# A streaming encoder step: strip products in longer groups, value products between feature tiles, sums off TensorE, and other planning margins

## The chip, the cores and the metric

The kernel runs on one core of a Trainium2 chip, as one launch. TensorE (PE) multiplies matrices, VectorE (DVE), ScalarE (ACT) and GpSimd (POOL) do the elementwise work, and DMA queues, issued by SyncE (SP) and GpSimd, move data between HBM and the core's own memory. The metric is the device time of one execution in microseconds (us).

## The reference, cut to what matters

Two layers of an encoder trunk are evaluated for 256 prompt tokens and for 8 streams of 16 sample tokens. Together these are 384 token rows of 1024 features.

```python
for i in range(2):
    x = x + 0.5 * rms(swiglu(rms(x), ffn 1))
    x = x + rms(conformer_conv(rms(x)) if i == 0 else gated_deltanet(rms(x)))
    x = x + rms(memory_cross_attention(rms(x), mem_k[i], mem_v[i]))
    x = x + 0.5 * rms(swiglu(rms(x), ffn 2))

def conformer_conv(h):                  # layer 0's mixer
    val, gate = split(h @ w_in + b_in)  # 1024 features each
    u = val * sigmoid(gate)
    c = depthwise_conv(u, 31 taps) + dw_b
    c = silu(layer_norm(c))             # mean and variance over the 1024 features
    return c @ w_out + b_out

def memory_cross_attention(h, k, v):    # 4 heads of 256, 256 memory tokens
    return softmax((h @ wq) k^T / 16) v @ wo
```

The memory keys and values of the prompt (`mem_prompt @ xa_wk`, `mem_prompt @ xa_wv`, both layers) are outputs too. The sample streams have their own keys and values, read from caches. The delta mixer of layer 1 keeps a 128 x 128 state per head and stream. All data is fp32.

## The kernel before, in words

Token tile 0 holds the 8 sample streams, tiles 1 and 2 the prompt. Each weight comes from HBM as a chunk of 128 x 1024 (`get`): SyncE loads it to `raw`, ScalarE copies it to `whi` in the type fp32r, and VectorE subtracts to get the rest, `wlo`. For chunks named in `SLOW`, GpSimd does that subtraction. A product is then three passes, high by high, high by low and low by high. Activations are split likewise into `hTh` and `hTl` (the normed input, turned so that features lie on partitions) and `rbh` and `rbl`. Products in plain fp32, such as the prompt's keys, are one product in the code and two matmul records in the trace. They stand as `ps<-big`.

Python generators emit operations with rough costs, and `Scheduler` orders all of them. It knows a cost for each operation, a delay from engine to engine (`LAT`), slots for DMAs, and then fixes one order for each engine. `early` places operations forwards by priority, `late` backwards; passes alternate, and the best end is kept. An engine on the chip runs its own order without exception and waits where data is late. So constants in the planner change the order and nothing else.

The names that the change touches:

- `quad` emits a set of four products side by side in four strips of 32 columns of the array (L265 in the trace), since each sample stream has its own keys. A head of the cross-attention has four sets for the scores and four for the values (two groups of streams, two halves of the contraction). A head of the delta mixer has two, for the state. Before, each set is an operation of its own to the planner, which may put other products between sets.
- `conv` emits eight feature tiles (a gate product `cg` and a value product `cv`, 24 passes of 384 columns each), then `glu` for each. The task `taps` takes the tiles in pairs: 31 taps each on VectorE, accumulated in PSUM. After each pair two products with a matrix of 1/1024 (`onesd`) add to the mean.
- `ln` normalises one token tile: subtract the mean (VectorE), square (ScalarE), eight products with `onesd` for the variance, power on GpSimd, a product that broadcasts it, multiply, SiLU.
- `kv_split` makes the prompt's values, as eight units of 48 passes of 256 columns, each with two weight chunks `v2`. It first splits the memory into `rbh` and `rbl`. Before, it runs behind the eighth feature tile.
- `kv(n)` emits n key products (each eight fp32 products of 256 columns) at places given by `KV`, where TensorE would wait for the norms between blocks.
- `chain` is the norm between two blocks, with its transposes on TensorE (L285).

Of the kernel before, what the change touches and what calls it, by code (L numbers as in the profile page):

```python
# [11 lines left out]
ALU = mybir.AluOpType  # L12
# [3 lines left out]
P = 128  # L16
D = 1024
KT = 8
NTOK = 384
# [17 lines left out]
RUSH = 10000.0  # L37
FIRST_SLOW = 2
ORD = 12000.0
# [5 lines left out]

KV = {"start": 3, "f00": 3, "conv": 5, "co": 2, "xo": 0, "f01": 1, "f10": 2, "dn": 0, "f11": 0}
HALF = 1400.0
GROUPS = [(0, 1), (2, 3, 4, 5, 6, 7)]
TAIL = 3
PASSES = 3  # L50
POOLTRUE = 1
LANES = 8
DMA_IN, DMA_OUT = 650.0, 950.0
# [47 lines left out]
class Emitter:  # L101
# [154 lines left out]
    def quad(self, mms):  # L256

        n = self._n(mms[0][2])
        cost = 2 * max(107.0, n / 1.2) + 190.0
        self.vt += cost  # L260
        t = self.nc.tensor

        def go():
            for out, lhsT, rhs, start, stop in mms:
                t.matmul(out, lhsT, rhs, start=start, stop=stop)  # L265
        self._add("P", cost, go, [x for m in mms for x in m[1:3]], [m[0] for m in mms])
        return self.vt + HOP
# [55 lines left out]
class Scheduler:  # L323

    LAT = {"P": {"P": 0, "A": 197, "V": 197}, "A": {"P": 275, "V": 131, "G": 159, "A": 131},
           "V": {"P": 260, "A": 128, "V": 127, "G": 155}, "G": {"P": 311, "A": 77, "V": 76, "G": 104}}

# [112 lines left out]
    def early(self, prio):  # L442
# [12 lines left out]
        for _ in ops:  # L455
            best, e, i = self.pick(free, now, later, lambda i: -prio[i])
            o = ops[i]
            cost = o.cost
            if o.nbytes:
                best = max(best, lanes[e][0])  # L460
            at[i] = best
            if o.table and o.table != table:
                table = o.table
                cost += 1283.0
            end = free[e] = best + cost
            if o.nbytes:
                dma = max(dma, end + DMA_IN) + o.nbytes / 360.0
                end = dma + DMA_OUT
                lanes[e] = lanes[e][1:] + [end]
            last = max(last, end)  # L470
            for j in o.succ:
                rd[j] = max(rd[j], end + (0.0 if o.nbytes else self.LAT[e].get(ops[j].eng, 150)))
                npred[j] -= 1
                if not npred[j]:
                    heapq.heappush(later[ops[j].eng], (rd[j], j))
# [66 lines left out]
class Model:  # L542
# [399 lines left out]
    def kv_split(self):  # L942


        E = self.E
        vt = E.vt
        mh, ml = (a.rearrange("p k c -> p (k c)")[:, 0:2 * D] for a in (self.rbh, self.rbl))
# [13 lines left out]
        for l in range(2):  # L961
            for h in range(XH):

                o, b = self.bank()
# [14 lines left out]
                self.bfree(b)  # L979
                E.store(self.O["pkv"][l, h][:, 512:1024], r)  # L980
        self.free(rh)
        E.vt = vt

# [76 lines left out]
    def conv(self, chains, post, pre):  # L1060
# [31 lines left out]

        def taps():
            for c0 in range(0, KT, 2):
                cs = (c0, c0 + 1)
# [24 lines left out]
                self.bfree(ab)  # L1120
                if not means:
                    means.append((yield from self.gbank()))
                for c in cs:
                    self.free(hist[c][1], hist[c][3])
                    E.mm(means[0][0][:, 0:NTOK], self.onesd, cO[:, c, :], c == 0, c == KT - 1)
            self.conv_end = e

        means = []
        tapper = E.spawn(taps())
        prefetch(0)  # L1130
        prefetch(1)
        for c in range(KT):
# [9 lines left out]
            if c + 2 < KT:  # L1142
                prefetch(c + 2)

        self.kv_split()
        self.kv(KV["conv"])
# [8 lines left out]
        def ln(t, dep):  # L1155
# [10 lines left out]
            yield e - 300  # L1166
            e = E.act(qv, x, AF.Square, dep=e)
            yield e
            o, b = yield from self.gbank()
            for k in range(KT):  # L1170
                e = E.mm(o[:, 0:P], qv[:, k, :], self.onesd, k == 0, k == KT - 1)
            v, r = self.st(1), self.st(1)
# [33 lines left out]
    def xattn(self, l, chains, post, pre):  # L1206
        E = self.E
# [14 lines left out]
        def head(h):  # L1222
# [3 lines left out]
            pk = unit[h, "p"][0]  # L1226
            sc, scb = yield from self.gbank2()
            for g in range(2):
                for c in range(2):
                    q4 = []  # L1230
                    for j in range(4):
# [3 lines left out]
                                   c == 0, c == 1))  # L1235
                    e0 = E.quad(q4)
            for t in (1, 2):
# [32 lines left out]
            yield max(e, e1, unit[h, ("v", 3)][2])  # L1270
            pv, pvb = yield from self.gbank2()
            for g in range(2):
                for m in range(2):
                    q4 = []
                    for j in range(4):
# [3 lines left out]
                        q4.append((pv[0][32 * j:32 * j + 32, g * MEM:(g + 1) * MEM], pt[:, o:o + 32], vv, m == 0, m == 1))  # L1279
                    e0 = E.quad(q4)  # L1280
            for d in range(2):
# [80 lines left out]
    def deltanet(self, chains, post, pre):  # L1362
# [119 lines left out]
        def head(h, q, k, v):  # L1482
# [136 lines left out]
            o, b = yield from self.gbank()  # L1619
            for n, a in ((0, kT), (256, qT)):  # L1620
                e = E.quad([(o[32 * j:32 * j + 32, n:n + 256], a[:, 32 * j:32 * j + 32], S[:, 256 * j:256 * j + 256], True, True)
                            for j in range(4)])

# [300 lines left out]
```

## Time and profile before

| | us |
|---|---|
| median of three runs | 1880.22 (1877.89 to 1883.22) |
| the profiled execution | 1880.99 |
| its span, first to last instruction | 1879.2 |
| PE busy | 1848.6 (98%) |
| DVE busy | 986.4 (52%) |
| ACT busy | 765.5 (41%) |
| POOL busy | 252.6 (13%) |

The stages on the span are: first feed-forward to about 305, convolution to about 512, first cross-attention to about 626, two feed-forwards to about 1186, delta mixer to about 1480, second cross-attention to about 1600, last feed-forward.

In the profile, a row of the timeline gives start, length, engine, line, operation, what is written and read, shape, count, and in brackets the idle time of the engine before it and what ended it. Matmuls overlap, so a single one's length is longer than the time until the next may start. That time is read from start to start.

### The profile page before, as it was taken

What the parts mean: (1) busy time and instruction counts of PE and PEld (TensorE: products, weight loads), DVE (VectorE), ACT (ScalarE), POOL (GpSimd) and SP (SyncE); (2) the same over time, 40 slices, a digit from 0 to 9 for tenths busy, and PEclk for the clock granted to TensorE, in tenths of its full rate; (3) what the DMA queues carried; (4) which work ended last, traced back from release to release, by engine and by line L of the source; (5) the groups of instructions that cost most, each with busy time, mean ns of one, the idle gap of its engine ahead of it and who ended that gap; (6) DMA issues with size and microseconds to landing.
All of it is one profiled execution on the core that took longest, in us unless ns stands there. A gap on an engine that the chain in (4) does not pass through costs nothing.

```text
span 1879.2 us, 26770 instructions
## 1 busy us (share of the span) xinstructions
PE 1848.6 (98%) x10479; PEld 1658.3 (88%) x10479; DVE 986.4 (52%) x1681; ACT 765.5 (41%) x1443; POOL 252.6 (13%) x420
## 2 busy tenths in 40 slices
PE   8999999999999999999999999999999999999998
PEld 7988998998877799999899999899998777899997
DVE  5456335898542643333643333687877644533333
ACT  4332334334542532323533333676665544432332
POOL 1000003568100100000200000233231101000000
PEclk9999999999999999999999999999999999999999
DMA  8534435448487534444434344333334583534441
GB/s 303 163 119 128 135 113 148 128 141 258 165 302 275 153 113 129 128 124 134 155 114 128 120 131 124 107 102 104 103 118 154 193 328 108 157 124 124 135 123 45
DMA packets 88622, 279.81 MB, mean 149 GB/s; under 512 B 17904, under 2 KB 20464, under 8 KB 88496
## 3 DMA queue, kind: packets, MB, share of 16 engines
q1 hardware_dynamic: 86368, 272.47, 45.4%
q0 software_dynamic: 2128, 5.63, 0.9%
q8 instruction: 82, 1.34, 0.3%
q14 instruction: 44, 0.36, 0.1%
HBM read 266.14 MB, written 11.92 MB: 148 GB/s over the span
## 4 chain that ended last, share of the span: by engine, by line
PE 63%; ACT 2%; DVE 2%; DMA 1%; POOL 1%; issue 1%; DVEq 0%; POOLq 0%; ACTq 0%; SPq 0%
PE ps L253 60%; PE ps L265 2%; PE ps L285 2%; DMA raw<-in_w 1%; DVE wlo L203 1%; ACT big L196 1%; POOL stat L203 1%; DVE big L216 1%; ACT whi L195 1%; PE ps L278 0%; ACT L196 0%; ACT hTl L196 0%; DVE hTl L203 0%; ACT big L195 0%; POOL stat L210 0%
## 5 line engine op out<-in xcount | busy, mean ns | idle before, releaser
L203 DVE TENSOR_TENSOR wlo<-raw,whi 128x1024 fp32r<-128x1024 f32 x341 | 415.3, 1223 | 566.9 <-ACT whi L195 564.8
L195 ACT CAST whi<-raw 128x1024 fp32r<-128x1024 f32 x377 | 393.7, 1050 | 710.7 <-PE ps L253 615.3
L253 PE MATMUL ps<-hTh,whi 128*128 128x384 f32 (+1 forms) x1680 | 505.6, 341 | 1.7 <-ACT big L196 0.7
L253 PE MATMUL ps<-hTl,whi 128*128 128x384 f32 (+1 forms) x1680 | 501.7, 339 | 0.1
L253 PE MATMUL ps<-hTh,wlo 128*128 128x384 f32 x1680 | 500.1, 339 | 0.0
L253 PEld LDWEIGHTS ps<-hTh,whi 128*128 128x128 f32 x1680 | 309.7, 188 | 14.4 <-ACT big L196 6.1
L253 PEld LDWEIGHTS ps<-hTl,whi 128*128 128x128 f32 x1680 | 310.2, 188 | 10.3 <-issue 2.8
L253 PEld LDWEIGHTS ps<-hTh,wlo 128*128 128x128 f32 x1680 | 309.6, 188 | 5.9 <-issue 0.7
L253 PE MATMUL ps<-whi,rbh 128*128 128x512 f32 (+1 forms) x800 | 242.2, 379 | 2.4 <-DVE big L216 2.3
L253 PE MATMUL ps<-whi,rbl 128*128 128x512 f32 (+1 forms) x800 | 244.1, 378 | 0.0
L253 PE MATMUL ps<-wlo,rbh 128*128 128x512 f32 (+1 forms) x800 | 240.9, 377 | 0.6 <-POOL wlo L203 0.6
L253 PE MATMUL ps<-big 128*128 128x128 f32 (+3 forms) x1144 | 216.0, 316 | 9.4 <-DMA big<-in_w 6.8
L253 PEld LDWEIGHTS ps<-big 128*128 128x128 f32 x1144 | 178.6, 192 | 36.8 <-issue 13.0
L253 PEld LDWEIGHTS ps<-wlo,rbh 128*128 128x128 f32 x800 | 150.2, 189 | 26.6 <-issue 1.6
L253 PEld LDWEIGHTS ps<-whi,rbh 128*128 128x128 f32 x800 | 149.2, 189 | 26.0 <-ACT big L196 2.6
L253 PEld LDWEIGHTS ps<-whi,rbl 128*128 128x128 f32 x800 | 150.1, 189 | 22.4 <-issue 0.8
L210 POOL TENSOR_SCALAR stat<-stat 128x1 f32<-128x1 f32 (+2 forms) x48 | 17.6, 367 | 1023.1 <-ACT hTl L196 1004.5
L203 DVE TENSOR_TENSOR big<-big,ps 128x384 f32<-128x384 f32 (+4 forms) x131 | 67.4, 521 | 81.5 <-PE ps L253 64.3
L216 DVE SCALAR_TENSOR_TENSOR ps<-big,cols,ps 128x384 f32<-128x384 f32 (+12 forms) x232 | 107.4, 553 | 0.4
L203 POOL TENSOR_TENSOR wlo<-raw,whi 128x1024 fp32r<-128x1024 f32 x36 | 86.7, 2421 | 49.5 <-ACT whi L195 43.7
L253 PE MATMUL ps<-whi,hTh 128*128 128x512 f32 x240 | 86.6, 402 | 2.5 <-ACT hTh L195 2.1
L253 PE MATMUL ps<-whi,hTl 128*128 128x512 f32 x240 | 85.4, 400 | 0.0
(91 smaller groups left out, 1488.8 us busy)
## 6 DMA issues: line engine op xcount, KB each, us to landing
raw<-in_w SPq DMA_DIRECT2D x380, 512.0 KB, 4.0
big<-in_ck SPq DMA_DIRECT2D x32, 512.0 KB, 6.0
big<-in_cv SPq DMA_DIRECT2D x32, 512.0 KB, 6.0
big<-in_w SPq DMA_DIRECT2D x21, 512.0 KB, 6.4
big<-in_npre SPq DMA_DIRECT2D x8, 512.0 KB, 7.4
big<-in_npost SPq DMA_DIRECT2D x8, 512.0 KB, 6.5
big<-out_pkv SPq DMA_DIRECT2D x8, 512.0 KB, 5.8
big<-in_state SPq DMA_DIRECT2D x8, 512.0 KB, 4.4
```

The lines of the kernel that those rows point to most:

```text
L195: return self._on("A", cost, dep, lambda: sc.copy(out, in_), [in_], w)
L196: return self._on("A", cost, dep, lambda: sc.activation(out, in_, func, **kw), [in_, bias, scale] + ([] if after is None else [after]), w, ...
L203: return self._on(eng, cost, dep, lambda: e.tensor_tensor(out=out, in0=a, in1=b, op=op), [a, b], [out])
L210: return self._on(eng, cost, dep, lambda: e.tensor_scalar(out=out, in0=a, scalar1=s1, scalar2=s2, op0=op0, **kw), [a, s1, s2 if s2 is not ...
L216: lambda: v.scalar_tensor_tensor(out=out, in0=a, scalar=s, in1=b, op0=op0, op1=op1), [a, s, b], [out])
L253: self._add("P", cost, lambda: t.matmul(out, lhsT, rhs, start=start, stop=stop, **kw), [lhsT, rhs], [out])
L265: t.matmul(out, lhsT, rhs, start=start, stop=stop)
L285: self._add("P", 109.0, lambda: t.transpose(out, in_, ident), [in_, ident], [out])
```

## The change

Six edits go together.

1. `quad` takes several sets at once. A head's four sets for the scores are now one operation, as are its four for the values and the delta mixer's two, and nothing can be put between them.
2. The mean's sum over feature tiles 0 to 5 is done by GpSimd into `total` (five additions). TensorE then has three products, for `total` and for tiles 6 and 7.
3. The squares are first summed over the eight feature tiles on VectorE (`rsum`), and one product is left of eight per token tile.
4. `kv_split` becomes a generator, and one unit of it is emitted after each feature tile from `VFROM` = 2 on, the rest behind the eighth.
5. `FIRST_SLOW` goes from 2 to 4: the subtractions of four more chunks go to VectorE instead of GpSimd. In `KV` a key product moves from `f10` to `co`.
6. The planner's delays from ScalarE, VectorE and GpSimd to TensorE grow by 150 ns, a restart of TensorE after a wait costs 107 in it, and the cost of `quad` counts its sets.

```diff
-FIRST_SLOW = 2
+FIRST_SLOW = 4
+VFROM = 2
...
-KV = {"start": 3, "f00": 3, "conv": 5, "co": 2, "xo": 0, "f01": 1, "f10": 2, "dn": 0, "f11": 0}
+KV = {"start": 3, "f00": 3, "conv": 5, "co": 3, "xo": 0, "f01": 1, "f10": 1, "dn": 0, "f11": 0}
...
+RESTART = 107.0
...
         cost = 2 * max(107.0, n / 1.2) + 190.0
+        cost += (len(mms) // 4 - 1) * 2 * max(107.0, n / 1.2)
...
-    LAT = {"P": {"P": 0, "A": 197, "V": 197}, "A": {"P": 275, "V": 131, "G": 159, "A": 131},
-           "V": {"P": 260, "A": 128, "V": 127, "G": 155}, "G": {"P": 311, "A": 77, "V": 76, "G": 104}}
+    LAT = {"P": {"P": 0, "A": 197, "V": 197}, "A": {"P": 425, "V": 131, "G": 159, "A": 131},
+           "V": {"P": 410, "A": 128, "V": 127, "G": 155}, "G": {"P": 461, "A": 77, "V": 76, "G": 104}}
...
+            if e == "P" and best > free[e] + 10.0:
+                cost += RESTART
...
         for l in range(2):
             for h in range(XH):
+                yield
+                vt = E.vt
                 o, b = self.bank()
...
         def taps():
+            total, th = yield from self.galloc(NTOK)
...
-                if not means:
+                if c0 == KT - 4:
                     means.append((yield from self.gbank()))
                 for c in cs:
                     self.free(hist[c][1], hist[c][3])
-                    E.mm(means[0][0][:, 0:NTOK], self.onesd, cO[:, c, :], c == 0, c == KT - 1)
+                    if c == 1:
+                        E.tt(total, cO[:, 0, :], cO[:, 1, :], ALU.add, dep=e, eng="G")
+                    elif 1 < c < KT - 2:
+                        E.tt(total, total, cO[:, c, :], ALU.add, dep=e, eng="G")
+                    elif c >= KT - 2:
+                        E.mm(means[0][0][:, 0:NTOK], self.onesd, cO[:, c, :], False, c == KT - 1)
+                if c0 == KT - 4:
+                    E.mm(means[0][0][:, 0:NTOK], self.onesd, total, True, False)
...
             if c + 2 < KT:
                 prefetch(c + 2)
-        self.kv_split()
+            if c >= VFROM:
+                next(values, None)
+        for _ in values:
+            pass
         self.kv(KV["conv"])
...
             e = E.act(qv, x, AF.Square, dep=e)
+            qs, qsh = yield from self.galloc(P)
+            yield e
+            e = E.rsum(qs, q.rearrange("p (k c) -> p c k", k=KT), dep=e)
             yield e
             o, b = yield from self.gbank()
-            for k in range(KT):
-                e = E.mm(o[:, 0:P], qv[:, k, :], self.onesd, k == 0, k == KT - 1)
+            e = E.mm(o[:, 0:P], qs, self.onesd, True, True)
...
             sc, scb = yield from self.gbank2()
+            q4 = []
             for g in range(2):
                 for c in range(2):
-                    q4 = []
                     for j in range(4):
...
-                    e0 = E.quad(q4)
+            e0 = E.quad(q4)
```

The values' sets and the delta mixer's are grouped in the same way. The order of instructions shows three places.

TensorE in the first cross-attention. Before, the sets of one head stand in several runs (`x8` is two sets), with whole products between them:

```order
L253 MATMUL ps_102<-hTh,wlo_79 128x384
L265 MATMUL ps_101<-big 32x256 x8
L253 MATMUL ps_98<-big 128x256 x2
L265 MATMUL ps_101<-big 32x256 x4
L253 MATMUL ps_98<-big 128x256
L265 MATMUL ps_101<-big 32x256 x4
L253 MATMUL ps_98<-big 128x256
L265 MATMUL ps_99<-big 32x256 x8
L253 MATMUL ps_96<-big 128x256 x4
```

Now the same group is one row:

```order
L255 MATMUL ps_98<-hTh,wlo_80 128x384
L255 MATMUL ps_97<-hTh,whi_71 128x384
L269 MATMUL ps_101<-big 32x256 x16
L255 MATMUL ps_102<-big 128x256 x4
L255 MATMUL ps_103<-big 128x256 x4
```

In the whole program the sets stood in 48 runs and stand in 23 now, two of the groups side by side.

TensorE in the first feed-forward, where bank `ps_99` passes from one gate or up product to the next (ScalarE or VectorE reads it in between). Before:

```order
L253 MATMUL ps_99<-hTh,wlo_78 128x384
L253 MATMUL ps_103<-whi_72,rbl 128x512
L253 MATMUL ps_96<-whi_72,rbl 128x512
L253 MATMUL ps_97<-whi_72,rbl 128x512
L253 MATMUL ps_100<-hTl,whi_71 128x384
L253 MATMUL ps_100<-hTh,wlo_79 128x384
L253 MATMUL ps_98<-whi_72,rbl 128x512
L253 MATMUL ps_99<-hTh,whi_73 128x384
```

Now:

```order
L255 MATMUL ps_99<-hTh,wlo_83 128x384
L255 MATMUL ps_100<-hTh,wlo_84 128x384
L255 MATMUL ps_100<-hTh,whi_76 128x384
L255 MATMUL ps_100<-hTl,whi_76 128x384
...
L255 MATMUL ps_99<-hTh,whi_70 128x384
```

The three rows on `ps_100` come three times, so nine products of 384 columns stand between the two uses where four of 512 and two of 384 stood.

VectorE at the convolution's start. `rbl<-raw` is the second half of the memory's split, `big<-ps,cols,big` the gating of a feature tile, and `ps<-big,cols,ps` the taps. Before, the split stands inside the taps:

```order
L216 SCALAR_TENSOR_TENSOR ps_97<-big,cols,ps_97 128x384
L216 SCALAR_TENSOR_TENSOR ps_96<-big,cols,ps_96 128x384
L203 TENSOR_TENSOR rbl<-raw_87,rbh 128x1024
L216 SCALAR_TENSOR_TENSOR ps_97<-big,cols,ps_97 128x384
L216 SCALAR_TENSOR_TENSOR big<-big,cols,ps_96 128x384
```

Now it stands ahead of the first gating, among the last parts of the norm (`hTl`):

```order
L205 TENSOR_TENSOR rbl<-raw_87,rbh 128x1024
L205 TENSOR_TENSOR hTl<-ps_97,hTh 128x4x128
L205 TENSOR_TENSOR rbl<-raw_86,rbh 128x1024
L205 TENSOR_TENSOR hTl<-ps_98,hTh 128x4x128
L205 TENSOR_TENSOR wlo_80<-raw_88,whi_72 128x1024
L218 SCALAR_TENSOR_TENSOR big<-ps_99,cols,big 128x256
L218 SCALAR_TENSOR_TENSOR big<-ps_99,cols,big 128x8x16
L212 TENSOR_SCALAR ps_96<-big,cols 128x256
L205 TENSOR_TENSOR wlo_81<-raw_86,whi_73 128x1024
L218 SCALAR_TENSOR_TENSOR ps_96<-big,cols,ps_96 128x227
```

So both halves of the split moved out of the taps, and one weight split (`wlo_81`) came in.

More of the change, by code (lines that the diff above doesn't have):

```diff
@@ L945, in kv_split @@
         E = self.E
-        vt = E.vt
         mh, ml = (a.rearrange("p k c -> p (k c)")[:, 0:2 * D] for a in (self.rbh, self.rbl))
@@ L980, in kv_split @@
                 E.store(self.O["pkv"][l, h][:, 512:1024], r)
+                E.vt = vt
         self.free(rh)
-        E.vt = vt
     def early(self, what, order):
@@ L1124, in taps @@
                     self.free(hist[c][1], hist[c][3])
-                    E.mm(means[0][0][:, 0:NTOK], self.onesd, cO[:, c, :], c == 0, c == KT - 1)
+                    if c == 1:
[6 more added lines that the diff above has]
+                    E.mm(means[0][0][:, 0:NTOK], self.onesd, total, True, False)
+            self.free(th)
             self.conv_end = e
+        values = self.kv_split()
         means = []
@@ L1167, in ln @@
             e = E.act(qv, x, AF.Square, dep=e)
+            qs, qsh = yield from self.galloc(P)
+            yield e
+            e = E.rsum(qs, q.rearrange("p (k c) -> p c k", k=KT), dep=e)
             yield e
             o, b = yield from self.gbank()
-            for k in range(KT):
-                e = E.mm(o[:, 0:P], qv[:, k, :], self.onesd, k == 0, k == KT - 1)
+            e = E.mm(o[:, 0:P], qs, self.onesd, True, True)
+            self.free(qsh)
             v, r = self.st(1), self.st(1)
@@ L1271, in head @@
             pv, pvb = yield from self.gbank2()
+            q4 = []
             for g in range(2):
                 for m in range(2):
-                    q4 = []
                     for j in range(4):
@@ L1279, in head @@
                         q4.append((pv[0][32 * j:32 * j + 32, g * MEM:(g + 1) * MEM], pt[:, o:o + 32], vv, m == 0, m == 1))
-                    e0 = E.quad(q4)
+            e0 = E.quad(q4)
             for d in range(2):
@@ L1619, in head @@
             o, b = yield from self.gbank()
-            for n, a in ((0, kT), (256, qT)):
-                e = E.quad([(o[32 * j:32 * j + 32, n:n + 256], a[:, 32 * j:32 * j + 32], S[:, 256 * j:256 * j + 256], True, True)
-                            for j in range(4)])
+            e = E.quad([(o[32 * j:32 * j + 32, n:n + 256], a[:, 32 * j:32 * j + 32], S[:, 256 * j:256 * j + 256], True, True)
+                        for n, a in ((0, kT), (256, qT)) for j in range(4)])
             o3, b3 = yield from self.gbank()
```

## The prediction, made before the changed kernel ran

> **What bounds the kernel now.** I read the page first, then the windows of single stages, then TensorE's own timeline at the places that the change touches, then its waits.
>
> ```profile
> PE 1848.6 (98%) x10479; PEld 1658.3 (88%) x10479; DVE 986.4 (52%) x1681; ACT 765.5 (41%) x1443; POOL 252.6 (13%) x420
> ...
> 660.00:905.00 245.00, 245.00 (x1285) 227.63 (x1284) 92.73 (x106) 80.13 (x111) 3.30 (x8) 1.00 0.41 127
> ...
> 370.00:400.00 30.00, 27.12 (x158) 25.97 (x157) 29.20 (x64) 8.91 (x12) 14.12 (x10) 0.94 0.34 101
> 400.00:430.00 30.00, 29.96 (x242) 29.22 (x241) 28.19 (x64) 14.74 (x20) 27.07 (x16) 1.00 0.69 199
> 430.00:456.00 26.00, 25.38 (x160) 22.99 (x159) 26.00 (x58) 9.51 (x13) 18.80 (x14) 1.00 0.88 250
> 535.00:600.00 65.00, 64.90 (x502) 46.50 (x501) 24.51 (x50) 24.92 (x63) 0.00 (x0) 1.00 0.90 335
> ```
>
> The columns of a window are its length, then the busy time of PE, PEld, DVE, ACT and POOL, the granted clock, the DMA share and GB/s. TensorE is the bound nearly everywhere: the feed-forward window 660 to 905 has no idle time. So a product taken off TensorE, or a break in its stream, is worth its full length. Only the convolution (370 to 456) has a second engine at its limit, VectorE, busy 83 of 86 us.
>
> **Part 1: the strip products.** A set is four products side by side, eight records at L265. Single sets, then a run of five, in TensorE's timeline:
>
> ```profile
> 548.16 0.64 PE L265 MATMUL ps<-big 128*32 128x256 f32 x8
> 548.73 0.70 PE L253 MATMUL ps<-big 128*128 128x256 f32 x2
> 549.36 0.64 PE L265 MATMUL ps<-big 128*32 128x256 f32 x8
> ...
> 581.24 2.37 PE L265 MATMUL ps<-big 128*32 128x256 f32 x40
> 583.54 1.13 PE L253 MATMUL ps<-big 128*128 128x256 f32 x4
> ...
> 1192.43 3.19 PE L253 MATMUL ps<-big 128*128 128x256 f32 x14
> ...
> 1195.38 0.39 PE L253 MATMUL ps<-hTh,whi 128*128 128x256 f32 x1
> ```
>
> Matmuls overlap, so I count from start to start. A single set takes 548.73 - 548.16 = 0.57, five in a row 583.54 - 581.24 = 2.30, so each further set (2.30 - 0.57)/4 = 0.43 and 0.14 is paid once per run. The whole product after a set takes 549.36 - 548.73 = 0.63; seven such products in a row take 1195.38 - 1192.43 = 2.95, 0.42 each, so entering and leaving cost it another 0.21. A run's break costs 0.35 us. The order counts 48 runs before and 23 now (25 fewer): 25 x 0.34 = -8.5 us. If only the 0.14 is saved it is -3.5. Sets per program stay the same, and nothing hides a break on an engine that has no idle time.
>
> **Part 2: sums off TensorE.** The mean's eight products of 384 columns become three (five fewer), and the squares' eight products of 128 columns per token tile become one (21 fewer). The first fence row is the last two mean products and what follows; the second is 22 square products with three others of 256 columns.
>
> ```profile
> 457.24 1.56 PE L253 MATMUL ps<-big 128*128 128x384 f32 x4 [1.08 <-DVE big L216]
> 458.34 0.57 PE L253 MATMUL ps<-whi,rbl 128*128 128x256 f32 x1
> 458.75 0.28 PE L253 MATMUL ps<-whi,rbh 128*128 128x256 f32 x1
> ...
> 461.29 5.95 PE L253 MATMUL ps<-big 128*128 128x256 f32 x50
> 467.07 0.39 PE L253 MATMUL ps<-ident,stat 128*128 128x128 f32 x2
> ...
> L239 DVE TENSOR_REDUCE big<-big 128x96 f32<-128x384 f32 x8 | 6.8, 850 | 0.0
> ...
> L203 POOL TENSOR_TENSOR wlo<-raw,whi 128x1024 fp32r<-128x1024 f32 x36 | 86.7, 2421 | 49.5 <-ACT whi L195 43.7 <-issue 5.5
> ```
>
> A mean product is between (458.34 - 457.24)/2 = 0.55 and (458.75 - 457.24)/2 = 0.75; at 0.62, five are -3.1. A square product is (467.07 - 461.29 - 3 x 0.42)/22 = 0.205; 21 are -4.3. In their place GpSimd gets five additions of 384 columns (2421 ns x 384/1024 = 0.9 us each, 2.4 at most), behind the subtractions, memsets and stores that stand on its queue; it loses four subtractions of 2.4 us, and the last two feature tiles go to TensorE directly, so no addition stands at the end of the chain. Its idle time covers them: cost 0; without that cover the total would be late by at most one addition, 0.9. VectorE gets three reductions of 1024 values: at L239's rate (850 ns for 384) 2.3 us each, at its rate for plain operations of that size (below) 1.2. Two of them now stand ahead of the first tile's variance, while that product shrinks by 1.4 us; TensorE's cover there is the key products, of which 30 stand between the mean and the output projection (16 before). I take +0.5, ends 0 and +2.
>
> **Part 3: the margins.** The planner's delays from another engine to TensorE grow by 150 ns, and a restart is charged. No instruction is added. In the first feed-forward a gate product waits for the bank that ScalarE's activation reads, once per tile; first and last of eleven such places, and two undisturbed products of 512 columns:
>
> ```profile
> 45.25 0.34 PE L253 MATMUL ps<-hTh,wlo 128*128 128x384 f32 x1
> 45.43 0.63 PE L253 MATMUL ps<-whi,rbl 128*128 128x512 f32 x2
> 46.12 0.45 PE L253 MATMUL ps<-hTh,whi 128*128 128x384 f32 x1
> 46.40 0.34 PE L253 MATMUL ps<-hTl,whi 128*128 128x384 f32 x1
> ...
> 175.16 0.39 PE L253 MATMUL ps<-whi,rbl 128*128 128x512 f32 x1
> 175.66 0.44 PE L253 MATMUL ps<-hTh,whi 128*128 128x384 f32 x1
> 175.94 0.34 PE L253 MATMUL ps<-hTl,whi 128*128 128x384 f32 x1
> ...
> 633.08 0.39 PE L253 MATMUL ps<-whi,hTh 128*128 128x512 f32 x1
> 633.31 0.39 PE L253 MATMUL ps<-wlo,hTh 128*128 128x512 f32 x1
> ```
>
> A product of 512 columns takes 0.23 undisturbed, here 0.69 for two and the wait, 0.50 for one and the wait, so the wait is 0.23 to 0.27; the product of 384 after it takes 0.28 where the one at 45.25 takes 0.18, another 0.10. Eleven times 0.36 is 4.0. The order now puts nine products of 384 columns (9 x 0.174 = 1.57) between the last use of the bank and the next, where four of 512 and two of 384 stood (1.26, with the wait 1.54). The wait is just covered: I take -4.0; if it is missed by a little, the 0.10 stays, -2.9; at worst 0.
>
> **Part 4: the convolution.** VectorE's and TensorE's timelines, and the clock:
>
> ```profile
> 332.99 0.74 DVE L216 SCALAR_TENSOR_TENSOR big<-ps,cols,big 128x256 f32<-128x256 f32 x2 [9.88 <-ACT big L196]
> ...
> 370.80 1.22 DVE L203 TENSOR_TENSOR rbl<-raw,rbh 128x1024 fp32r<-128x1024 f32 x1 [1.66 <-ACT rbh L195]
> ...
> 402.04 0.74 DVE L216 SCALAR_TENSOR_TENSOR big<-ps,cols,big 128x256 f32<-128x256 f32 x2 [1.81 <-ACT big L196]
> ...
> 456.54 1.17 DVE L216 SCALAR_TENSOR_TENSOR big<-big,cols,ps 128x384 f32<-128x384 f32 x2
> ...
> 372.69 0.35 PE L253 MATMUL ps<-whi,rbh 128*128 128x256 f32 x1 [2.33 <-DVE big L216]
> ...
> 374.30 0.39 PE L253 MATMUL ps<-wlo,rbh 128*128 128x256 f32 x1 [0.56 <-POOL wlo L203]
> ...
> 374.70:378.30 3.60, 3.60 (x17) 3.60 (x17) 3.60 (x11) 0.36 (x1) 0.00 (x0) 0.53 0.49 168
> ```
>
> TensorE loses 2.33 + 0.56 at the first value product, then 3.6 us at a clock of 0.53 (3.6 x 0.47 = 1.7), and 1.08 at the mean: 5.7 us. What it may win back is set by VectorE, which works from 332.99 to 457.71 (124.7 us) with 1.66 + 1.81 idle. In the new order both splits of the memory (1.22 each) stand ahead of that stretch, in the 9.88 us in which VectorE waits, and one weight split of 1.22 stands inside; the other three that GpSimd gives up fall outside. The taps can then end 1.66 + 1.81 + 1.2 = 4.7 us earlier against the first gate, and the value products, spread from the third feature tile on, can't all wait at one place. I take -4.0. The ends are -4.7 and +3: if features come slower than VectorE uses them (eight products' worth of taps, 124.7/8 = 15 us a tile, against 14 us for a feature tile with a value unit on TensorE), it could idle another 1.8 at each of its four pairs. The wait that comes next is the mean's for the last tap, some 2 us.
>
> The Trainium skill, "TensorE: Matmul & The Clock Gate", Part 1, says that the clock halves after an idle window of about 3.4 us, and advises against gaps over some 3 us. This trace disagrees: a gap of 2.33 and one of 0.56 were followed by a clock of 0.53. By the page the remaining wait costs its own length, sum as below; by the trace, one wait of 2.3 us more would cost 1.7, and the term would be -2.3.
>
> **Part 5: a key product moved.** One key product of eight (8 x 0.42 = 3.4 us, its weights' load with it) moves from before the delta mixer to behind the convolution. The work stays; its cover at the old place goes. There the row at 1195.38 above started 2.95 us after the seven key products began, with a gap of 0.16 us only, so TensorE may stand up to 3.4 us; the chain it waits for was ordered around that cover and may come earlier. I take +1.5 (0 to +3.4).
>
> **Sum:** -8.5 - 3.1 - 4.3 + 0.5 - 4.0 - 4.0 + 1.5 = -21.9. The profiled execution took 1880.99 (span 1879.2 and 1.8 around it), 0.8 above the median 1880.22: 1859.1 there, 1858 for a median.
>
> **Rivals.**
>
> ```profile
> PE ps L285 <- DVE big L216: 6.5, 8, 1.5
> ...
> PE ps L253 <- ACT hTh L195: 2.1, 2, 1.4
> ...
> SPq L289 <- PE ps L265: 22.6, 9, 6.6
> ...
>   PEld ps L265: 0.7, 2
> ```
>
> *Only the removed work counts* (0.20). Waits are set by chains and cover; taken away at one place they return at the next. Then -8.5 - 7.4, and +1.5 and +0.5: -13.9, 1866. For it: VectorE's limit in the convolution.
>
> *The margins cure more* (0.13). The first two rows are TensorE's waits for the norms between blocks, 8.6 us; with the short waits that end under 0.15 us, each with a restart of 0.10, half might go: another -6, 1852. Against it: these chains have little cover to be moved.
>
> *The waits come back in full* (0.11): another order of everything, with new waits of some 18 us: 1876. Against it: in the feed-forwards the trace has none to speak of.
>
> *Slower: the caches' loads* (0.05). The third row (SyncE's queue, 500 to 600 us) says that loads stood 22.6 us behind the strip products that free their buffers, at a DMA share of 0.90; the last that TensorE waited for those loads only 0.7 us. A merged group waits for all four loads and frees all four buffers at its end. If each head's loads start 3 us later and DMA is the limit there, eight heads cost 24 us and eat the gain: 1882. It decides from 2.7 us a head on.
>
> **How the numbers follow.** My sum has 0.51, with 1852 to 1865 from the ends of parts 2 to 5. The range 1846 to 1872 takes in the two rivals beside it and leaves out most of the last two. A difference under 0.3% (5.6 us) can't be told from none here. Below 1874.6 lie my sum, the first two rivals and a quarter of the third: 0.87; within 0.3% 0.08, slower 0.05.
>
> **What would show it.** Strip runs of 16 or 32 records at 0.43 a set, some 23 of them; three mean products together; waits of 0.25 us gone between 45 and 176 us; no clock below 1 near 375; a wait of about 2 us ahead of the mean. I am wrong if TensorE waits for cache loads or for VectorE in the convolution by more than 5 us, or if its busy time falls by less than 12.

## The result, and the profile after

The changed kernel takes 1854.24 us (median of 4 runs, 1853.36 to 1854.83), the kernel before 1879.39 on the same chip (4 runs). The ratio is 0.9863, 95% interval 0.9846 to 0.9880: 25 us faster. Forecast was 1858.0. The profiled execution took 1854.83, span 1853.0, which is 26.2 less than the span before.

The page's busy times and windows of the stages, columns as before:

```profile
PE 1828.5 (99%) x10427; PEld 1653.1 (89%) x10427; DVE 992.6 (54%) x1688; ACT 769.1 (42%) x1443; POOL 244.5 (13%) x421
...
370.00:400.00 30.00, 29.88 (x201) 29.07 (x200) 30.00 (x69) 11.47 (x16) 23.50 (x16) 1.00 0.54 150
400.00:430.00 30.00, 30.00 (x229) 29.50 (x228) 30.00 (x70) 10.54 (x15) 21.34 (x19) 1.00 0.62 173
430.00:456.00 26.00, 25.42 (x134) 21.43 (x133) 24.47 (x36) 11.73 (x16) 19.55 (x14) 1.00 0.85 295
...
374.70:378.30 3.60, 3.60 (x27) 3.60 (x26) 3.60 (x8) 1.05 (x1) 2.77 (x2) 1.00 0.29 60
```

TensorE's busy time fell by 20.1. In the convolution VectorE no longer pauses until the last tap, and where the clock stood at 0.53 before (374.70 to 378.30) it is 1.00, with 27 products in place of 17. The strips in TensorE's timeline, now 32 records at a time:

```profile
520.88 1.93 PE L269 MATMUL ps<-big 128*32 128x256 f32 x32
522.74 1.56 PE L255 MATMUL ps<-big 128*128 128x256 f32 x6
...
529.86 1.93 PE L269 MATMUL ps<-big 128*32 128x256 f32 x32
531.73 3.72 PE L255 MATMUL ps<-big 128*128 128x256 f32 x16
```

Four sets take 1.86 from start to start. VectorE's timeline, with the second half of the memory's split, the first gate, the last tap, and the subtraction of the mean:

```profile
314.93 1.23 DVE L205 TENSOR_TENSOR rbl<-raw,rbh 128x1024 fp32r<-128x1024 f32 x1 [1.23 <-ACT rbh L197]
...
324.08 0.74 DVE L218 SCALAR_TENSOR_TENSOR big<-ps,cols,big 128x256 f32<-128x256 f32 x2 [0.48 <-ACT big L198]
...
443.66 0.61 DVE L218 SCALAR_TENSOR_TENSOR big<-big,cols,ps 128x384 f32<-128x384 f32 x1
445.38 1.22 DVE L205 TENSOR_TENSOR big<-big,ps 128x1024 f32<-128x1024 f32 x1 [1.10 <-PE ps L255]
```

From first gate to end of the last tap: 444.3 - 324.1 = 120.2 us, where it was 124.7. TensorE's timeline at four places: two transposes of the norm ahead of the convolution, the mean, the first output projection, and a product of the second cross-attention:

```profile
307.96 0.60 PE L289 MATMUL ps<-ident,big 128*128 128x128 f32 x4
...
311.36 0.66 PE L289 MATMUL ps<-ident,big 128*128 128x128 f32 x4
...
444.33 6.09 PE L255 MATMUL ps<-big 128*128 128x384 f32 x26 [0.18 <-DVE big L218]
...
464.30 0.50 PE L255 MATMUL ps<-whi,hTh 128*128 128x512 f32 x1 [1.01 <-ACT hTh L197]
...
1528.65 1.99 PE L255 MATMUL ps<-big 128*128 128x256 f32 x8 [2.05 <-DMA big<-out_pkv]
```

The transposes no longer wait. Before, in TensorE's timeline, they did:

```profile
311.36 0.66 PE L285 MATMUL ps<-ident,big 128*128 128x128 f32 x4 [1.51 <-DVE big L216]
...
320.11 1.38 PE L285 MATMUL ps<-ident,big 128*128 128x128 f32 x8 [1.29 <-DVE big L216]
```

The mean waits 0.18 for the last tap (1.08 before). New are a wait of 1.01 behind the mean and one of 2.05 for a load.

**One account for the runs.** (The two with added products are left out, since their work differs.) I take the starts of all TensorE records of a trace. "Work" prices each record at the median distance to the next start that its kind has in the trace of before; "breaks" is 0.337 us for each run of strips (from the starts: 0.233 beyond 0.431 a set, and 0.104 on the product behind it); "rest" is what is left: waits, restarts, low clock. The three and some 11.5 us at both ends make the span.

| kernel | timed median | traced span | work | breaks | rest |
|---|---|---|---|---|---|
| before | 1879.4 | 1879.2 | 1795.2 | 16.2 | 56.4 |
| after | 1854.2 | 1853.0 | 1787.4 | 7.8 | 46.2 |
| sets_single | 1869.4 | 1869.2 | 1787.4 | 15.5 | 54.8 |
| margins_old | 1856.4 | 1855.0 | 1787.4 | 7.8 | 48.5 |
| sums_old | 1867.1 | 1864.0 | 1795.2 | 7.8 | 49.2 |
| values_old | 1903.7 | 1896.5 | 1787.4 | 7.8 | 89.9 |
| values_late | 1897.0 | 1896.7 | 1787.4 | 7.8 | 89.9 |
| split_on_gpsimd | 1857.0 | 1855.8 | 1787.4 | 7.8 | 49.0 |
| key_back | 1860.7 | 1858.0 | 1787.4 | 7.8 | 51.5 |
| sets_alone | 1876.0 | 1870.9 | 1795.2 | 7.8 | 56.4 |
| margins_alone | 1873.5 | 1872.4 | 1795.2 | 15.2 | 50.5 |
| sums_alone | 1886.1 | 1886.1 | 1787.4 | 16.2 | 71.0 |

So the change took 7.8 of work, 8.4 of breaks and 10.2 of rest. Of the rest, 4.0 lie in the start and the first feed-forward, 3.2 at the norm ahead of the convolution, 6.2 in the convolution; 2.2 came back behind the mean and about 1 elsewhere.

Each run was timed beside the kernel before, whose median was between 1878.3 and 1880.8 in these sessions (1879.4 beside the changed kernel). So a difference below of two timed medians, one of them the changed kernel's, is good to some 2 us.

### The profile page after: what moved, and what is told of

The parts are those of the page before. It is cut to its first block, busy times and chain, and to the rows that moved or that the text cites. A ratio compares the mean times of both kernels' runs of the same rounds, so it can differ in the third digit from the quotient of the medians.

```text
span 1853.0 us, 26684 instructions
## 1 busy us (share of the span) xinstructions
PE 1828.5 (99%) x10427; PEld 1653.1 (89%) x10427; DVE 992.6 (54%) x1688; ACT 769.1 (42%) x1443; POOL 244.5 (13%) x421
## 4 chain that ended last, share of the span: by engine, by line
PE 80%; DVE 10%; ACT 4%; DMA 2%; issue 2%; POOL 2%; SPq 0%; DVEq 0%; POOLq 0%; ACTq 0%
PE ps L255 76%; DVE ps L218 6%; PE ps L289 2%; PE ps L269 2%; ACT big L198 2%; DVE big L218 1%; DMA raw<-in_w 1%; ACT whi L197 1%; POOL stat L205 1%; DVE wlo L205 1%; DVE big L205 1%; DMA big<-out_pkv 1%; DMA big<-in_w 0%; ACT L198 0%; DVE big L241 0%
## 5 line engine op out<-in xcount | busy, mean ns | idle before, releaser
L255 PE MATMUL ps<-hTh,whi 128*128 128x384 f32 x1680 | 509.8, 339 | 1.6 <-ACT big L198 0.6
L255 PE MATMUL ps<-hTl,whi 128*128 128x384 f32 (+1 forms) x1680 | 508.8, 338 | 0.4 <-DVE hTl L205 0.3
L255 PE MATMUL ps<-whi,rbl 128*128 128x512 f32 (+1 forms) x800 | 239.0, 377 | 0.0
L255 PE MATMUL ps<-big 128*128 128x128 f32 (+3 forms) x1092 | 198.9, 316 | 11.0 <-DMA big<-in_w 6.3
L255 PEld LDWEIGHTS ps<-big 128*128 128x128 f32 x1092 | 169.8, 192 | 32.5 <-DMA big<-in_w 7.0
L218 DVE SCALAR_TENSOR_TENSOR ps<-big,cols,ps 128x384 f32<-128x384 f32 (+14 forms) x232 | 108.0, 561 | 0.4
L255 PE MATMUL ps<-wlo,hTh 128*128 128x512 f32 x240 | 84.2, 393 | 0.0
```

What stands on the lines that cost most here:

```text
L218: lambda: v.scalar_tensor_tensor(out=out, in0=a, scalar=s, in1=b, op0=op0, op1=op1), [a, s, b], [out])
L255: self._add("P", cost, lambda: t.matmul(out, lhsT, rhs, start=start, stop=stop, **kw), [lhsT, rhs], [out])
```

## Experiments

Two theories stand throughout: A, each part is worth its TensorE time and the waits that it is named for; B, the gain is an order of everything that happens to fit, so that undoing any part may cost anything.

**The sets.** One run undoes the merging (the scores' place is shown; the values, the delta mixer and the cost in `quad` go back likewise):

```diff
-            q4 = []
             for g in range(2):
                 for c in range(2):
+                    q4 = []
                     for j in range(4):
...
-            e0 = E.quad(q4)
+                    e0 = E.quad(q4)
```

> The changed kernel with one part undone: in the cross-attention and the delta mixer every set of strips is again its own step. The order counts 46 runs of strips in place of 23. Theory A (each part is worth its TensorE time): 23 runs x 0.35 us = 8.1 us more than the changed kernel's 1854, so 1862; strip-related waits of TensorE rise from 9.8 us back towards 17. If leaving a run costs only the 0.14: 1857.5. Theory B (most of the gain is a lucky order of everything, and any new plan moves the time by several us either way): any time from 1848 to 1872, with differences spread over stages that have no strips.

sets_single took 1869.4 us, ratio to before 0.9957 (0.9941 to 0.9972): 15.2 slower than the changed kernel, more than A said. The account has 7.7 of breaks, as A, and 8.6 of rest. A part of that rest belongs to the strips. Four sets in a row stopped in their middle, in TensorE's timeline:

```profile
571.26 1.49 PE L268 MATMUL ps<-big 128*32 128x256 f32 x20
575.42 1.33 PE L268 MATMUL ps<-big 128*32 128x256 f32 x12 [2.68 <-DMA big<-in_ck]
```

The price of a break by itself comes from a pair with the same work in the same order, where only the place of three added products in a group differs (shown for the scores; the values have the same):

```diff
+                    if g + c < 2:
+                        q4.insert(0, (sc[1][:, 0:MEM], qT[:, 2 * h, 0:P], unit[h, ("k", 0)][0][:, 0:MEM], True, True))
```

In the second of the two, `append` stands for `insert(0`, so that each product follows a set.

> The changed kernel with three more whole products of 256 columns in each of the 16 cross-attention groups (8 heads, scores and outputs, both tiles of layers together), ahead of the group's four sets. Their results are overwritten by products that follow, so nothing else changes. It is the control for the run beside it. 48 products at 0.42 us: 20 us more than the changed kernel, about 1874 for both theories, if TensorE has no idle time there; 24 runs of strips.

> The same 48 products, one between each set and the next, so that the order counts 71 runs of strips in place of 24 and is otherwise the same on every engine. Theory A (a run of strips costs 0.34 us for entering and leaving, 0.23 of it before the next whole product starts and 0.10 on that product): 47 x 0.34 = 15.8 us slower than the run with the products in front. If only the 0.14 of the prediction is paid: 6.6 us. Theory B (what single sets cost is their effect on the order of everything, not the break): the two are equal within 2 us.

With the products in front the time was 1877.6 (some 1874 was expected), in between 1894.5: 16.9 more (16.2 between the two traces), where 15.8 was expected for 47 breaks. The same group in TensorE's timeline, first in front, then in between:

```profile
519.27 0.42 PE L255 MATMUL ps<-hTh,wlo 128*128 128x384 f32 x1
519.53 3.32 PE L269 MATMUL ps<-big 128*128 128x256 f32 x38
522.78 1.99 PE L255 MATMUL ps<-big 128*128 128x256 f32 x8
```

```profile
519.48 0.42 PE L255 MATMUL ps<-hTh,wlo 128*128 128x384 f32 x1
519.83 4.23 PE L269 MATMUL ps<-big 128*32 128x256 f32 x38
523.99 1.99 PE L255 MATMUL ps<-big 128*128 128x256 f32 x8
```

3.25 against 4.16 us for the group, and 0.26 against 0.35 for the product ahead of it: 1.00 more for three breaks (1.006 in the median of the groups), 0.335 each. The price is shown.

The kernel before with the sets merged and nothing else:

> The kernel before with one part of the change alone: the sets of a group as one step (23 runs of strips in place of 48). Theory A: 25 x 0.337 = 8.4 us faster, 1871 to 1872, with TensorE's other waits unchanged within 2 us. Rival (the run with single sets was 15 us slower than the changed kernel, of which breaks explain 7.8; if the rest belongs to the sets too, through loads of the caches that come late): 1864 to 1867.

sets_alone took 1876.0 (12 runs, 1871.7 to 1878.3), ratio 0.9978 (0.9969 to 0.9987): 3.5 faster, not 8.4. The profiled execution is one of the fastest of them (1872.7), and its account is A's to the tenth: breaks 8.4 less, rest equal. But the traced execution of before is slow for its kernel (span 1879.2, where the median of the 18 beside sets_alone is 1877.8). And the typical execution of sets_alone is slower than its trace. The granted clock of each execution is listed with its time: the three at 0.999 have spans of 1869.9 to 1871.1 us, the nine at 0.996 to 0.998 spans of 1872.7 to 1876.5. A mean clock lower by 0.002 would be worth 0.002 x 1871 = 3.7 us where TensorE is the bound. So stretches of low clock are a likely part of the answer; where they fall isn't in any trace, and the rest of the gap stays open.

**The margins.** Undone in the changed kernel, and alone on the kernel before:

```diff
-    ... "A": {"P": 425, ...}, "V": {"P": 410, ...}, "G": {"P": 461, ...}
+    ... "A": {"P": 275, ...}, "V": {"P": 260, ...}, "G": {"P": 311, ...}
-            if e == "P" and best > free[e] + 10.0:
-                cost += RESTART
```

> The changed kernel with the planner's old delays (150 ns shorter towards TensorE) and without the charged restart. No instruction differs, only the order. Theory A (the waits of the first feed-forward, 4.0 us, are what the margins cure): 1858, with waits of about 0.25 us back between 45 and 176 us and little elsewhere. The rival that the margins cure more (the norms' waits between blocks, 8.6 us before and 4.0 now, and short waits after the second strip stage): 1862 to 1866. Theory B (luck): the first feed-forward is as it was changed, and the difference falls anywhere.

> The kernel before with the planner's larger delays and the charged restart alone. In the first feed-forward the order now puts 1.49 us of products between two uses of a bank, where it was 1.26 (the product times of the trace). Theory A (a wait is there where the cover is under about 1.5): ten or eleven waits of 0.28 gone, 35 to 180 us shorter by 3 to 4 us, and 1876 in all. Rival (undoing the margins in the changed kernel cost only 2 us, so they cure nothing by themselves): 1879 to 1881.

Undone they cost 2.1 (1856.4, ratio 0.9882, 0.9863 to 0.9901, which overlaps the change's own interval); alone they gain 6.0 (1873.5, ratio 0.9964, 0.9952 to 0.9977). The window of the eleven waits, 45 to 176 us, where the count of TensorE's products shows what the waits take: before, after, margins_old and margins_alone:

```profile
45.00:176.00 131.00, 129.32 (x668) 117.59 (x667) 73.37 (x150) 41.37 (x55) 0.00 (x0) 1.00 0.45 138
```

```profile
45.00:176.00 131.00, 130.35 (x686) 121.30 (x685) 77.61 (x153) 44.46 (x55) 0.00 (x0) 1.00 0.46 147
```

```profile
45.00:176.00 131.00, 131.00 (x688) 121.47 (x687) 76.67 (x153) 43.72 (x55) 0.00 (x0) 1.00 0.46 147
```

```profile
45.00:176.00 131.00, 130.52 (x684) 120.89 (x685) 76.57 (x152) 42.95 (x56) 0.00 (x0) 1.00 0.47 146
```

668 products became 686, and 688 without the margins. So the margins alone cure most of these waits: nine of the eleven are gone, at six places a restart of 0.11 stays, and the rest of 35 to 180 us falls by 1.9 where 3 to 4 was expected. The other part of their gain lies elsewhere (1.0 of it in breaks, since this order has 45 runs of strips in place of 48). But in the changed kernel another part's order does the same as the margins: there the order with the old delays leaves 1.56 us of products between two uses of the bank at nine of the first ten places, at the product times of the trace. Neither part owns those 4 us.

**The sums.**

```diff
-                    if c == 1:
-                        E.tt(total, cO[:, 0, :], cO[:, 1, :], ALU.add, dep=e, eng="G")
...
+                    E.mm(means[0][0][:, 0:NTOK], self.onesd, cO[:, c, :], c == 0, c == KT - 1)
...
-            e = E.rsum(qs, q.rearrange("p (k c) -> p c k", k=KT), dep=e)
+            for k in range(KT):
+                e = E.mm(o[:, 0:P], qv[:, k, :], self.onesd, k == 0, k == KT - 1)
```

> The changed kernel with the mean's sum and the squares' sums again on TensorE (eight products of 384 columns, eight of 128 columns for each token tile). Theory A: TensorE's busy time rises by 3.1 + 4.3 = 7.4 us, VectorE loses three reductions, and the time rises by 6.9 to 7.4, to 1861.5. The rival that the first tile's reductions stand on the path between mean and output projection (that stretch grew from 16.3 to 19.5 us with the change): the rise is smaller than the busy time's, 3 to 5 us, to 1858. Theory B: anything from 1850 to 1870.

sums_old took 1867.1, ratio 0.9939 (0.9923 to 0.9955), 12.8 slower, beyond A and the rival: work 7.8, near A, and rest 3.0 in a traced run that was 1.3 under the median. The rest grew by 4.0 in the convolution: value products stood earlier there, and VectorE idled 6.0 once between two pairs.

> The kernel before with the sums taken off TensorE alone. Two things in the order matter: TensorE has 7.8 us less work, and in the first feed-forward only 0.87 us of products stand between two uses of a bank, where it was 1.26. Theory A (cover theory, and the mean waits for VectorE's last tap whatever TensorE saves ahead of it): the eleven waits grow from 0.28 to about 0.67, +4.3 us; the mean's products save nothing, the squares' 4.3: about 1880 in all, no change. Rival (work taken off a full TensorE counts in full): 1872 to 1873, or 1877 with the longer waits.

sums_alone took 1886.1, ratio 1.0034 (1.0022 to 1.0046): 6.5 slower than before with 7.8 us less work, and 6 above A's 1880. The count in the first window falls as A said:

```profile
45.00:176.00 131.00, 126.90 (x656) 115.79 (x655) 73.10 (x150) 42.27 (x54) 0.00 (x0) 1.00 0.43 136
```

The waits there grew from 0.28 to 0.51 each, for 0.39 less cover. And in the convolution TensorE stood twice for some 3 us:

```profile
394.74 0.39 PE L253 MATMUL ps<-wlo,rbh 128*128 128x256 f32 x1 [2.97 <-POOL wlo L203]
...
411.29 0.39 PE L253 MATMUL ps<-whi,rbh 128*128 128x256 f32 x1 [3.16 <-DVE big L216]
```

From first gate to last mean product it took 126.1 us (125.3 before), so the mean's saving bought nothing: in the convolution TensorE had 4.8 us less work and 6.4 more rest, part of it half clock behind each of these two waits (last section). That work off a full engine counts in full is refuted for this part alone. But the account has 14.6 us more rest in all, and the other 8 lie in other stages, so the new order that theory B speaks of has a share in this loss.

**The value products between the tiles.** First all of it undone, then the block alone, then the weight splits alone:

```diff
-VFROM = 2
+VFROM = 99
-FIRST_SLOW = 4
+FIRST_SLOW = 2
```

> The changed kernel with the value products again as one block behind the last feature tile, and the first features' planning of before. Theory A (the spread value products cover TensorE's waits and keep the clock up): a gap of about 2 us at the first value product, then a clock near 0.5 for some 3.6 us as before, and 4 us to 7 us more in all (5.5 us of the gain stood between the first feature tile and the mean), so 1858 to 1861. Rival (the splits' new places and the sums do it, the spread is hidden anyway): within 1 us of 1854, with the last mean product at the same time.

> The changed kernel with the value products again in one block behind the last feature tile, and nothing else undone (the split of the third and fourth feature tile's weights stays on VectorE). Theory A (the block itself takes VectorE's turn: ScalarE's seed for the taps stands behind the block's copies, and VectorE idles some 20 us at the third or fourth pair): VectorE idle by 15 to 25 us between 395 and 425, the last mean product at about 475 to 482 instead of 445, 1885 to 1904. Rival (the planning of the first feature tiles' splits did it): 1854 to 1860.

> The changed kernel with the weights of the third and fourth feature tile split on GpSimd again, as before the change, and the values between the tiles as changed. Theory A (VectorE's chain from the first gate to the last tap sets when the mean comes, and these splits lie outside it): within 1.5 us of 1854. Rival (they are what made 49 us of difference in the run with old values): 1890 to 1904.

values_old took 1903.7 (ratio 1.0128, 1.0108 to 1.0149), values_late 1897.0 (1.0089, 1.0067 to 1.0112) and split_on_gpsimd 1857.0 (0.9885, 0.9857 to 0.9913). The first was far from both expectations; the next two place nearly all of it in the block. values_late, in VectorE's timeline, in ScalarE's, and in TensorE's:

```profile
398.50 0.61 DVE L218 SCALAR_TENSOR_TENSOR big<-big,cols,ps 128x384 f32<-128x384 f32 x1
418.30 0.55 DVE L212 TENSOR_SCALAR ps<-big,cols 128x256 f32<-128x256 f32 x1 [19.19 <-ACT ps L197]
```

```profile
417.53 0.37 ACT L197 COPY big<-ps 128x256 f32<-128x256 f32 x1 [2.41 <-PE ps L255]
417.94 0.27 ACT L197 COPY ps<-big 128x128 f32<-128x128 f32 x1
```

```profile
475.93 4.42 PE L255 MATMUL ps<-big 128*128 128x256 f32 x11 [19.42 <-DVE big L218]
```

The eight feature tiles are done at 396, no later than before (400). But ScalarE's short copy that seeds the next pair's taps in PSUM (417.94) stands in its queue behind the value units' casts and copies, which wait for loads and for TensorE. VectorE idles 19.2, and TensorE pays it back at the mean with 19.4 and a low clock behind it. The last mean product comes at 483.8 where it came at 444.8. In every run that product stands 120 to 131 us behind the first gate once VectorE's pauses are taken out (after 120.7, before 121.8, sums_old 126.6, values_late 130.4; what differs is other work on VectorE). So the place of the value products isn't worth 4 us but keeps VectorE's chain whole; before, the same block happened to be ordered with a pause of only 3.5.

**The key product.**

```diff
-KV = {... "co": 3, ..., "f10": 1, ...}
+KV = {... "co": 2, ..., "f10": 2, ...}
```

> The changed kernel with the key product moved back from behind the convolution to the place ahead of the delta mixer. The work is the same. The prediction's step (its cover at the delta mixer is missed, +1.5 us by the move): 1852.7, with the 3.6 us of waits ahead of the first strips of the delta mixer smaller. Rival (the cover is worth more behind the convolution, where TensorE still waits 2.2 us between the mean and the output projection): 1855 to 1858, with that wait longer by 1 to 3 us.

key_back took 1860.7, ratio 0.9896 (0.9883 to 0.9909): 6.5 slower, a little beyond the rival. Behind the mean TensorE runs dry, in its timeline and in the window of what follows:

```profile
463.70 0.39 PE L255 MATMUL ps<-rbl,ones_r 128*128 128x512 f32 x1
467.79 0.80 PE L255 MATMUL ps<-whi,hTh 128*128 128x512 f32 x1 [3.69 <-ACT hTh L197]
...
467.79:470.94 3.15, 3.15 (x7) 2.48 (x8) 2.34 (x2) 3.15 (x6) 1.22 (x1) 0.50 0.62 163
```

The wait is 3.69 against 1.01, and half clock follows it (3.4 us in the trace's clock record, of which the window shows 3.15), another 1.7. Ahead of the delta mixer the rest is 3.4 with the product back and 3.6 without it.

## Why the prediction was right or wrong

| step | predicted | measured in the traces |
|---|---|---|
| Part 1, breaks | -8.5 | -8.4 |
| Part 2, work | -7.4 | -7.8 |
| Part 2, VectorE's reductions | +0.5 | +2.2 of rest between mean and output projection, in great part ScalarE's order (below) |
| Part 3, eleven waits | -4.0 | -3.7 (rest of 35 to 180 us: 5.9 to 2.2) |
| Part 4, convolution | -4.0 | -6.2 |
| Part 5, key product | +1.5 | +0.1 of rest ahead of the delta mixer |
| not in the sum | | -3.2 at the norm ahead of the convolution, +0.8 start, ends and others |
| sum | -21.9 | -26.2 |

*Part 1* held to the tenth, with its price confirmed by the pair (0.335; the working gives 0.35, the sum takes 0.34). But the saved breaks show in full only in a trace: timed alone the part gave 3.5.

*Part 2* had the work right and its condition wrong. "TensorE is the bound nearly everywhere" was read from windows, and in the convolution the same rows had VectorE at its limit; there sums_alone got nothing for the mean's five products. Alone the part loses 6.5 us. In the whole change the work came off in full; that this needed the shorter chain of Part 4 is argued, since no run has these two parts alone. The reductions on VectorE, priced at 1.2 to 2.3 us, in the groups by shape:

```profile
L241 DVE TENSOR_REDUCE big<-big 128x128 f32<-128x1024 f32 x3 | 5.7, 1931 | 0.0
```

At 1.93 each they are a small part of what lengthened the stretch from the last mean product to the output projection from 16.3 to 19.5 us. VectorE's multiplication of the first tile starts 9.3 us into it before and 9.7 now. Behind that stands ScalarE, in its timeline before and after:

```profile
468.82 3.58 ACT L196 ACTIVATE big<-big,cols 128x128 f32<-128x128 f32 x9 [2.81 <-DVE big L203]
472.30 1.03 ACT L195 CAST hTh<-big 128x1024 fp32r<-128x1024 f32 x1
```

```profile
455.75 1.28 ACT L198 ACT_TABLE_LOAD   x1 [1.83 <-DVE big L205]
457.05 6.27 ACT L198 ACTIVATE big<-big,cols 128x128 f32<-128x128 f32 x16
463.22 1.98 ACT L197 CAST hTh<-big 128x1024 fp32r<-128x1024 f32 x2
```

It now loads a table behind the multiplication (1.3; ahead of it in every run with the sums on TensorE), and it does 16 pieces of the SiLU ahead of the first cast of `hTh`, where it did 9 (2.7 more). The 16 pieces don't come from the reductions. sums_old has 16 pieces and no reductions: its stretch is 18.4 us and ends with a wait of 1.74. sums_alone has the reductions and 9 pieces: 16.8 us and a wait of 0.13. So the +0.5 was near for the reductions; ScalarE's order behind them is what the term left out.

*Part 3* had the size right and the cause half right: the waits went and the margins alone cure most of them, but the margins aren't needed for it in the changed kernel.

*Part 4* is the mis-sized term. Its limit of 4.7 for the taps against the first gate was met nearly exactly (125.3 to 120.7 us up to the last mean product, 4.6). What failed is "the wait that comes next is the mean's, some 2 us": it is 0.18, and the clock stayed at 1. The -3.2 ahead of it belong to the rival on the norms' waits: 1.5 and 1.3 us of them went. That rival had the place right and the cause wrong: without the margins they are gone as well, with the margins alone they aren't (from the first feed-forward's last product to the last of the first feature tile: 23.8 before, 21.5 after, 21.9 margins_old, 23.6 margins_alone). None of the three parts tried alone removes them (23.6 to 24.0), and of the runs made from the changed kernel only values_old has them (24.8), while values_late and split_on_gpsimd, which undo half of that edit each, haven't (20.3, 21.5). More than one order removes them, and which step of the change does stays open.

*Part 5* has the wrong sign. I priced the cover that is lost at the old place and gave nothing for the cover gained at the new one. The product there fills time in which TensorE would stand, so the move is worth some 5 us (6.5 timed), while the old place didn't miss it.

Of the rivals, "only the removed work counts" (1866) is refuted, since the rest fell by 10.2. "The waits come back in full" describes sums_alone, not the change. "Slower: the caches' loads" didn't come: TensorE waits for no load of the sample streams' caches. Its wait of 2.05 us in the second cross-attention (1528.65 above) is for the prompt's keys or values read back from `out_pkv`; it was single sets that met a wait of 2.68 for a cache (`in_ck`).

Theory A explains the work and the breaks. Theory B is too strong as it stands, since margins_old and split_on_gpsimd change the order alone or nearly so and move the time by 2 and 3 us, but sums_alone shows that an order can cost several us. And the parts don't add. The five undone one by one (sets, margins, sums, values, key product) cost 15.2 + 2.1 + 12.8 + 49.5 + 6.5 = 86 us, the whole 25. So each seems to rely on an order that the others leave; no run undoes or adds two of them together, so this is argued and not shown.

## What to carry to other kernels

Before work taken off the busiest engine is booked at its full length, look in its own stage for the chain that the stage ends on: where another engine's chain is at its limit, the saving turns into a wait. Book a moved filler at both ends, the cover lost and the cover gained. And when a planner sets the order, look at the small instruction that starts the limiting chain (here a copy of 0.27 us) and at what stands ahead of it in its queue.

## What the hardware showed that I had not expected

*The clock.* Idle gaps of 2.05 (after, 1528.65) and 1.01 left TensorE's clock at 1.00; those of 3.69 (key_back) and 19.42 us (values_late) were followed by 3.4 and 3.6 us at 0.50, the second in this window:

```profile
475.93:479.50 3.57, 3.57 (x9) 2.85 (x9) 3.57 (x8) 0.00 (x0) 1.99 (x2) 0.50 0.00 0
```

The Trainium skill, "TensorE: Matmul & The Clock Gate", Part 1, puts the limit at an idle window of about 3.4 us that runs free of the program. These gaps agree with it. The traces' clock records fit a window that runs free, too: apart from the one at a kernel's end, every stretch at 0.50 lasts 3.41 us or a whole multiple of it, and the three of sums_alone (395.10, 412.16 and 1217.71) start 5 and 236 times 3.413 us apart.

That the whole window must be idle doesn't agree. In before, 2.33 and 0.56 with 1.0 us of products between them were enough (the 0.53 is 3.41 us at 0.50 and the rest at 1.00). So was the gap of 2.68 in sets_single (575.42 above), and so were those of 2.97 and 3.16 in sums_alone. The windows behind the three:

```profile
576.10:579.45 3.35, 3.35 (x13) 2.30 (x10) 0.56 (x2) 0.53 (x2) 0.00 (x0) 0.50 1.02 418
```

```profile
395.12:398.50 3.38, 3.38 (x19) 3.38 (x18) 3.38 (x9) 1.32 (x2) 1.46 (x1) 0.50 0.55 165
...
412.20:415.55 3.35, 3.35 (x18) 3.35 (x17) 3.35 (x9) 1.72 (x3) 3.35 (x3) 0.50 0.45 115
```

In sets_alone half clock came in the delta mixer with no gap over 0.47 us in the 7 us ahead of it, behind products of 8 columns. TensorE's timeline and the window:

```profile
1204.91 0.83 PE L253 MATMUL ps<-big 128*128 128x8 f32 x6 [0.47 <-DVE big L216]
...
1207.40:1210.70 3.30, 3.30 (x18) 3.30 (x17) 3.15 (x12) 3.25 (x5) 0.74 (x2) 0.50 0.00 0
```

How much idle or narrow work in a window is enough, no run here measures.

*Strips.* Going from 128 columns to strips of 32 and back costs 0.335 us, and hardly depends on the number of sets: what a run takes beyond 0.43 a set is 0.14 for one set (548.16 before) and 0.14 for four (520.88 after). The Trainium skill, "TensorEngine Tiling (Array Packing)", Key Properties, says that a change of the tiling mode drains TensorE; the pair of runs is in line with that and gives the price; the drain itself isn't seen in a trace.

*A restart.* The first product after a wait, or after strips, takes 0.10 us more than its kind (0.28 in place of 0.17 for 384 columns, at 46.12 of before), even where the wait itself is too short to be seen as idle time: in margins_alone a product at 83.40, some 0.05 late, takes 0.29.
